# A fourth buffer for the "acc" tiles of an input projection, and late raw tiles placed in the rows pool

## The chip, the cores and the metric

The kernel runs on one core of a Trainium2 chip. The time is the device time of one execution in microseconds (us). The profile is that of one execution; its times count from the start of the recorded span. Engines: PE is TensorE (matrix products), DVE is VectorE, ACT is ScalarE, POOL is GpSimd, and SP is the engine whose queue issues the transfers (DMA).

## The reference

One layer of an encoder block for x of 2048 tokens by 1024 channels, in float32: a pre-norm, one input projection to ten groups of columns, a pooling branch, a bidirectional mLSTM branch, gates, an output projection and a post-norm. Cut to what the change touches:

```python
h = rms_norm(x, norm_pre_g)
proj = jnp.einsum('bsd,de->bse', h, w_in)
u_a, z_a, q, k, v, o, z_b, gates, g_a, g_b = jnp.split(proj, split_points, axis=-1)
pooled = multiscale_pool(u_a)              # window means minus the token, windows 2, 4, 8, 16
y_a = (mix(pooled) * pool_scale) * silu(z_a)
qk = silu(centred_depthwise_conv(concat([q, k]), conv_qk_w, conv_qk_b))   # 5 taps along the tokens
...                                        # mLSTM of q, k, v and the gates, both directions
y_b = hb * sigmoid(o) * silu(z_b)
merged = sigmoid(g_a + b_merge[0]) * (y_a @ w_proj_pool) + sigmoid(g_b + b_merge[1]) * (y_b @ w_proj_mlstm)
out = x + rms_norm(merged @ w_out, norm_post_g)
```

## The kernel before

The function `phase1` is the input projection. It goes over the tokens in two halves of 1024 and, in each, over 36 pairs of 128-column blocks (q, k, v, pooled u, gates z, o and others, by head or group). A pair's product with the half of the tokens is done by Strassen's scheme: seven products, each of 12 matmuls of 128x512 (4 blocks of depth times 3, as each factor is split in a high and a low part). The sums gather in PSUM banks A, B and C, two of each. In `strassen`, S2·T2 goes to a bank B; DVE reads it (L395, tile `u2`); S3·T3 is added in the same bank; DVE reads it again (L400, `u3`); A22·T4 is added, and DVE's L705 or L595 adds the bank to `p1` (to tiles `p` or `raw`). So PE can't go on in the bank until L395, then L400, are done. The products of neighbouring pairs are interleaved: PE runs S3·T3 of a pair 8 us after its S2·T2 ended.

What follows a pair depends on its kind. All of these take tiles of the tag "acc", 128 partitions by up to 1048 floats, from one ring of three buffers:

- `conv` (q, k): ACT writes acc = bias + tap 0 (L623), DVE adds four taps (L628), ACT takes the sigmoid (L632), POOL multiplies (L633), SP stores (L634, to qT or kT).
- `pair_v`: two tiles `vnh` and `vnl` for each half of the pair, with MEMSETs (L647, L648) at their first use, PE transposes (L654, to `vtr`), ACT's and DVE's split into high and low part (L94, L98), and SP's stores.
- `pair_u`: window sums `win` (L685) and `pooled` (L689 to L695).
- `pair_o` and `pair_z`: gate tiles `gB` (L754 to L760) and `zs` (L719 to L724).

A tile of the ring is handed out when the tile three places earlier has been released, that is, when its last reader is done: for a convolution, when its store has landed.

In the second half, convolutions are left over from the first: the second block of each q and k pair needs tokens of both halves, so its raw values were spilled. `late_load` brings one back into a tile `late` (a MEMSET, L638, and a load, L639), and `conv` is run on it after a later pair that is no q, k, u or v. Its taps are tied by `issue_after` to the bank reads of that pair, so that bank reads and taps alternate on DVE. There are eight: q0, k0, q1, k1, q2, k2, q3, k3.

Ahead of the seventh pair of the second half, `row_math` computes the row factors of the mLSTM in the tile `rows`, of tag "rb" in the pool `self.rows` (one buffer).

The order on each engine is not written out by hand: a scheduler sets it from the priorities in the code (`tc.high_priority`, `issue_after`) and from when it reckons tiles to come free. Engines run their instructions in that order.

Of the kernel before, what the change touches and what calls it, by code (L numbers as in the profile page):

```python
# [8 lines left out]
F32 = mybir.dt.float32  # L9
# [4 lines left out]
P = 128  # L14
# [3 lines left out]
HALF = S // 2  # L18
# [54 lines left out]
def run(steps):  # L73
    for _ in steps:
        pass


class Kernel:
# [358 lines left out]
    def phase1(self):  # L437
        tc, nc, a = self.tc, self.nc, self.a
        with ExitStack() as es:
# [7 lines left out]
            po = {t: es.enter_context(tc.tile_pool(name=f"po_{t}", bufs=3)) for t in ("raw", "acc", "p")}  # L447
            self.rows = es.enter_context(tc.tile_pool(name="rows", bufs=1))
            self.decay = es.enter_context(tc.tile_pool(name="decay", bufs=1))
            self.late = es.enter_context(tc.tile_pool(name="late", bufs=1))  # L450
            psum = es.enter_context(tc.tile_pool(name="ps1", bufs=2, space=bass.MemoryType.PSUM))

            class PoolP:
                def tile(s_, shape, dt, tag, name, bufs=None):
                    return po.get(tag, po["p"]).tile(
                        shape, dt, tag=tag, name=name, bufs=bufs or (6 if tag == "p" else 3)
                    )

            pool = PoolP()
# [2 lines left out]
            late, waits = [(kind, h) for h in range(NH) for kind in "qk"], None  # L462
            for half in range(2):
                H = {}
                ops = self.operands(half, H, hp, wc, pool, psum)
                def load(i):
                    return [self.load_w(wr, i, slice(4 * j, 4 * j + 4)) for j in range(2)]

                def work(i, W):
                    return self.pair(half, self.pairs[i], H, W, psum, pool)  # L470


                self.half = half
                W = [{}, {}]
                ahead = lambda: tc.high_priority(offset=NEXT if half else 0)
                with ahead():
                    next(ops)
                    raw = [self.load_w(wr, i, slice(0, 4)) for i in range(2)]
                    if half == 0:
                        raw.append(self.load_w(wr, 0, slice(4, 8)))  # L480
                    next(ops)
                    for i in range(2):
                        self.plain_w(W[i], wc, raw[i], 1, "pool")
                    next(ops)
                    for i in range(2):
                        if len(raw) < 3 + i:
                            raw.append(self.load_w(wr, i, slice(4, 8)))
                        self.plain_w(W[i], wc, raw[2 + i], 2, "pool")
                    if wg is None:
                        wg = self.prep_wg(pool)  # L490
                    next(ops)
                both = []
                for i in range(2):
                    self.plain = ("AB", ("CC", "AB")[i])
                    both.append(work(i, W[i]))
                    next(both[i])
                self.plain = None
                gates = self.gates(half, H, wg, psum, pool)
                for _ in range(KT):
                    next(gates, None)  # L500
                    for g in both:
                        next(g)
                with tc.issue_after(self.evac.ins):
                    next(ops)
                for _ in range(KT):
                    next(gates, None)
                    for g in both:
                        next(g, None)
                run(gates)
                for g in both:  # L510
                    run(g)
                run(ops)
                rest = iter(())
                for i in range(2, n):
                    if half == 1 and i == 6:
                        self.row_math(psum)
                        mask = self.decay.tile([P, 2, P], F32, tag="mask", name="mask", bufs=1)
                        nc.sync.dma_start(mask, a["mask"])
                    if half == 0 and i == 8:
                        self.stats(1, pool)  # L520
                    self.edge = i == n - 1
                    W = {}
                    with tc.high_priority(offset=200):
                        if half == 0:
                            with tc.issue_after(self.scaled[8].ins) if i == 2 else ExitStack():
                                self.prep_w(W, load(i), wc, wt)
                        else:
                            self.again_w(W, i, wr, wc)
                    if half == 1:
                        with tc.issue_after(self.read.ins):  # L530
                            for u in range(max(0, 8 * (i - 10) // 6), max(0, min(32, 8 * (i - 9) // 6))):
                                self.masked(u, mask)
                    if half == 0:
                        self.keep_w(W, i)


                    this, self.read_banks = work(i, W), []
                    next(this)
                    next(rest, None)
                    next(this)  # L540
                    run(rest)
                    next(this)
                    rest = this
                    if half == 1 and waits is not None and i >= 7 and self.pairs[i][0] not in "qkuv":
                        kind, h, raw = waits
                        self.conv(pool, kind, h, 1, raw, HALF - 2, 0, self.read_banks)
                        waits = None
                    elif half == 1 and waits is None and late and i >= 5:
                        with tc.issue_after(self.read.ins):
                            waits = self.late_load(*late.pop(0))  # L550
                run(rest)
# [82 lines left out]
        nc.sync.dma_start(self.sp[f"{kind}T{h}"][:, i, tstart : tstart + n], acc[:, :n])  # L634

    def late_load(self, kind, h):
        raw = self.late.tile([P, HALF + 2], F32, tag="late", name=self.nm("late"))
        self.nc.vector.memset(raw[:, 0:2], 0.0)  # L638
        self.nc.sync.dma_start(raw[:, 2:], self.sp[f"raw{kind}{h}"])  # L639
        return kind, h, raw  # L640
# [932 lines left out]
```

## Time and profile before

| | |
|---|---|
| runs | 2403.22, 2401.22, 2403.05 us; median 2403.05 |
| profiled execution | 2403.61 us, of which the span is 2401.8 |
| mean granted clock of PE | 0.989 |
| busy share of the span | PE 97%, DVE 62%, POOL 48%, ACT 37% |
| input projection, first half, second half, the rest | about 0 to 780, 780 to 1472, 1472 to 2402 us |

A row of a timeline gives the start, the duration, the engine, the line, the operation, the tiles written and read, their size and number, and in brackets the engine's idle time before it with what ended it. "SPq" is SP's queue issuing a transfer. A row of waits says who waited for which instruction: us in total, times, longest.

### The profile page before, as it was taken

The page shows a single profiled execution, that of the slowest core. Times are in us where ns is not written, and L with a number is a line of the kernel's source. Part 1 is how long each engine was busy: PE and PEld are TensorE (multiplying, and loading weights), DVE is VectorE, ACT ScalarE, POOL GpSimd, SP SyncE. Part 2 cuts the span into 40 slices and gives each one's busy share as a digit, 9 for nine tenths or more (in the row PEclk, how much of TensorE's full clock was granted, in tenths as well). Part 3 has the DMA queues.
Part 4 walks back from the last instruction along what each step waited for, and adds up shares of the span by engine and source line. Part 5 has one row for each costly group of instructions (what it writes and reads, how often), then busy time and mean ns, then how long its engine had stood idle before and what let it go on. Part 6 is the DMA issues. An engine that isn't in the chain of part 4 may idle for free.

```text
span 2401.8 us, 35786 instructions
## 1 busy us (share of the span) xinstructions
PE 2321.7 (97%) x12569; PEld 2004.0 (83%) x12569; DVE 1480.2 (62%) x2495; ACT 895.1 (37%) x1773; POOL 1147.0 (48%) x902
## 2 busy tenths in 40 slices
PE   7999999999999989999999999998999999999998
PEld 5787888888887878787878887997989999999776
DVE  6876676677656465565656434887875333354865
ACT  5434333433344333322322333765764212121442
POOL 4655564555545333554664530554554211233775
PEclk9999999999999999999999999998999999999999
DMA  4467656565673566788777866776666546588763
GB/s 150 176 221 266 225 207 236 201 234 210 235 260 126 185 179 215 250 263 272 241 244 248 267 221 245 236 207 204 198 184 201 187 154 197 184 286 276 253 221 123
DMA packets 303011, 521.63 MB, mean 217 GB/s; under 512 B 27504, under 2 KB 138224, under 8 KB 302832
## 3 DMA queue, kind: packets, MB, share of 16 engines
q1 hardware_dynamic: 302832, 519.35, 65.1%
q8 instruction: 99, 1.62, 0.3%
q14 instruction: 80, 0.66, 0.1%
HBM read 318.45 MB, written 200.80 MB: 216 GB/s over the span
## 4 chain that ended last, share of the span: by engine, by line
PE 67%; DMA 11%; DVE 10%; POOL 4%; issue 4%; ACT 3%; SPq 1%; POOLq 0%; DVEq 0%; ACTq 0%
PE bankB L106 6%; PE bankB L107 6%; PE bankB L108 6%; PE bankC L107 4%; PE bankC L106 4%; PE bankC L108 4%; PE bankA L108 4%; PE bankA L107 4%; PE bankA L106 4%; PE num L1213 4%; DVE acc L628 3%; PE pb L922 2%; PE pb L921 2%; PE pb L923 2%; DMA negM<-nm 2%
## 5 line engine op out<-in xcount | busy, mean ns | idle before, releaser
L98 POOL TENSOR_TENSOR wB21l<-wraw,wB21h 128x512 fp32r<-128x512 f32 x76 | 110.1, 1449 | 223.3 <-ACT wB21h L94 181.0
L1197 POOL TENSOR_TENSOR qs<-q,isc 128x256 f32<-128x256 f32 x120 | 91.1, 761 | 152.5 <-PE num L1213 67.0
L628 DVE SCALAR_TENSOR_TENSOR acc<-raw,conv_w,acc 128x1026 f32<-128x1026 f32 (+1 forms) x96 | 153.3, 1610 | 11.3 <-ACT acc L623 8.9
L98 POOL TENSOR_TENSOR wB22l<-wraw,wB22h 128x512 fp32r<-128x512 f32 x76 | 121.8, 1602 | 73.2 <-ACT wB22h L94 51.5
L923 PE MATMUL pb<-oxs,w_proj_mlstml 128*128 128x256 f32 x512 | 143.8, 281 | 0.0
L922 PE MATMUL pb<-oxs,w_proj_mlstmh 128*128 128x256 f32 x512 | 143.8, 281 | 0.0
L921 PE MATMUL pb<-oxs,w_proj_mlstmh 128*128 128x256 f32 x512 | 143.5, 280 | 0.0
L922 PE MATMUL paps<-pys,w_proj_poolh 128*128 128x256 f32 x512 | 142.7, 281 | 0.3 <-POOL pys L98 0.3
L923 PE MATMUL paps<-pys,w_proj_pooll 128*128 128x256 f32 x512 | 141.4, 281 | 0.0
L921 PE MATMUL paps<-pys,w_proj_poolh 128*128 128x256 f32 x512 | 141.3, 280 | 0.0
L98 POOL TENSOR_TENSOR wB11l<-wraw,wB11h 128x512 fp32r<-128x512 f32 x72 | 105.4, 1464 | 47.6 <-ACT wB11h L94 46.8
L106 PE MATMUL bankB<-A22h,wT4h 128*128 128x512 f32 x272 | 107.1, 394 | 9.5 <-DVE u L400 9.4
L106 PE MATMUL bankC<-S1h,wT1h 128*128 128x512 f32 x272 | 107.0, 393 | 3.4 <-ACT sg L739 3.4
L905 POOL TENSOR_TENSOR nm<-nm,mask 128x256 f32<-128x256 f32 x64 | 63.5, 1007 | 93.1 <-DMA nm<-negM 86.4
L395 DVE TENSOR_TENSOR u<-bankB,p 128x512 f32<-128x512 f32 x76 | 52.1, 686 | 90.4 <-PE bankB L108 78.0
L108 PE MATMUL bankB<-S2h,wT2l 128*128 128x512 f32 x272 | 106.5, 391 | 1.1 <-DVE wT2l L98 1.1
L106 PE MATMUL bankB<-S3h,wT3h 128*128 128x512 f32 x272 | 106.2, 390 | 1.3 <-DVE u L395 1.3
L107 PE MATMUL bankB<-S2l,wT2h 128*128 128x512 f32 x272 | 107.3, 395 | 0.0
L108 PE MATMUL bankC<-S1h,wT1l 128*128 128x512 f32 x272 | 106.9, 393 | 0.0
L107 PE MATMUL bankC<-S1l,wT1h 128*128 128x512 f32 x272 | 106.9, 393 | 0.0
L106 PE MATMUL bankA<-A12h,wB21h 128*128 128x512 f32 x272 | 106.7, 392 | 0.0
L108 PE MATMUL bankB<-A22h,wT4l 128*128 128x512 f32 x272 | 106.6, 392 | 0.0
(443 smaller groups left out, 7751.6 us busy)
## 6 DMA issues: line engine op xcount, KB each, us to landing
wraw<-in_w_in SPq DMA_DIRECT2D x110, 512.0 KB, 4.3
wt<-wT2h SPq DMA_DIRECT2D x34, 256.0 KB, 4.6
wt<-wT1h SPq DMA_DIRECT2D x34, 256.0 KB, 4.4
wt<-wT3h SPq DMA_DIRECT2D x34, 256.0 KB, 3.6
wt<-wT2l SPq DMA_DIRECT2D x34, 256.0 KB, 4.2
wt<-wT1l SPq DMA_DIRECT2D x34, 256.0 KB, 4.4
wt<-wT3l SPq DMA_DIRECT2D x34, 256.0 KB, 3.4
wt<-wT4h SPq DMA_DIRECT2D x34, 256.0 KB, 2.2
```

Source lines behind the costliest of these rows:

```text
L98: return eng.tensor_tensor(lo, x, hi.bitcast(F32), op=ALU.subtract)
L106: nc.tensor.matmul(ps, wh, xh, start=start and kt == 0, stop=False, skip_group_check=True)
L107: nc.tensor.matmul(ps, wh, xl, start=False, stop=False, skip_group_check=True)
L108: nc.tensor.matmul(ps, wl, xh, start=False, stop=stop and kt == 3, skip_group_check=True)
L395: self.read_banks.append(nc.vector.tensor_tensor(u2, bank["B"], p1, op=ALU.add))
L628: nc.vector.scalar_tensor_tensor(acc[:, :n], raw[:, tap : tap + n], self.cw[:, ct, tap : tap + 1], acc[:, :n], op0=ALU.mult, op1=ALU.add,)
L905: nc.gpsimd.tensor_tensor(t[:, d, :, :], t[:, d, :, :], mask[:, d, None, :].to_broadcast([P, 2, P]), op=ALU.add)
L921: nc.tensor.matmul(ps, wh, xh, start=i == 0, stop=False)
L922: nc.tensor.matmul(ps, wh, xl, start=False, stop=False)
L923: nc.tensor.matmul(ps, wl, xh, start=False, stop=i == n)
L1197: nc.gpsimd.tensor_tensor(qs[d], q[:, :, ck], isc[:, d, j % 2, None, :].to_broadcast([P, 2, P]), op=ALU.mult)
L1213: nc.tensor.matmul(pn, qs[d][:, kt, :], state[:, kt, :], start=kt == 0, stop=False)
```

## The change

```diff
-            self.late = es.enter_context(tc.tile_pool(name="late", bufs=1))
...
                     return po.get(tag, po["p"]).tile(
-                        shape, dt, tag=tag, name=name, bufs=bufs or (6 if tag == "p" else 3)
+                        shape, dt, tag=tag, name=name, bufs=bufs or dict(p=6, acc=4).get(tag, 3)
                     )
...
-                    elif half == 1 and waits is None and late and i >= 5:
+                    elif half == 1 and waits is None and late and i >= 7:
                         with tc.issue_after(self.read.ins):
                             waits = self.late_load(*late.pop(0))
...
     def late_load(self, kind, h):
-        raw = self.late.tile([P, HALF + 2], F32, tag="late", name=self.nm("late"))
+        raw = self.rows.tile([P, HALF + 2], F32, tag="rb", name=self.nm("late"))
```

The acc ring has four buffers (4192 bytes more of each partition); the pool of the late tile (4104 bytes) is gone, and late tiles take the buffer in which the rows of `row_math` lay before. The first late load is issued two pairs later, after `row_math`; the other seven loads and all eight late convolutions stay at the same pairs. Tiles of tag "acc" now wait for the release of the tile four places earlier. Lines behind L455 move up by one (L628 becomes L627, L705 becomes L704).

PE's order does not change by a row. The instructions are the same on every engine; some of the first phase stand elsewhere. Two places on DVE:

The late convolution of k2 (tile acc_1738 before), with the bank reads of the pair around it (u2_1762 by L395 and u3_1763 by L400), before:

```order
L395 TENSOR_TENSOR u2_1762_10073<-bankB_1759_10045,p1_1761_10059 128x512
L705 TENSOR_TENSOR p1_1731_9887<-bankB_1729_9873,p1_1731_9887 128x512
L705 TENSOR_TENSOR u2_1732_9901<-bankC_1730_9874,u2_1732_9901 128x512
L628 SCALAR_TENSOR_TENSOR acc_1738_9995<-late_1684_9682,conv_w_376,acc_1738_9995 128x1022
L756 TENSOR_TENSOR gB_1737_9979<-u2_1732_9901,gB_1737_9979 128x512
L628 SCALAR_TENSOR_TENSOR acc_1738_9995<-late_1684_9682,conv_w_376,acc_1738_9995 128x1022 x2
L400 TENSOR_TENSOR u3_1763_10128<-bankB_1759_10045,p1_1761_10059 128x512
L628 SCALAR_TENSOR_TENSOR acc_1738_9995<-late_1684_9682,conv_w_376,acc_1738_9995 128x1022
```

The same place after:

```order
L395 TENSOR_TENSOR u2_1762_10070<-bankB_1759_10042,p1_1761_10056 128x512
L627 SCALAR_TENSOR_TENSOR acc_1738_9992<-late_1684_9679,conv_w_373,acc_1738_9992 128x1022 x2
L704 TENSOR_TENSOR p1_1731_9884<-bankB_1729_9870,p1_1731_9884 128x512
L627 SCALAR_TENSOR_TENSOR acc_1738_9992<-late_1684_9679,conv_w_373,acc_1738_9992 128x1022
L704 TENSOR_TENSOR u2_1732_9898<-bankC_1730_9871,u2_1732_9898 128x512
L627 SCALAR_TENSOR_TENSOR acc_1738_9992<-late_1684_9679,conv_w_373,acc_1738_9992 128x1022
L755 TENSOR_TENSOR gB_1737_9976<-u2_1732_9898,gB_1737_9976 128x512
L400 TENSOR_TENSOR u3_1763_10125<-bankB_1759_10042,p1_1761_10056 128x512
```

Two taps moved ahead of both L705, and all four stand ahead of L400, where one stood behind it.

The late convolution of k1 (acc_1570) and the sets of the values of head 2 (vnh_1622, vnl_1623, vnh_1626), before, from its first two taps on; L395 of this pair (u2_1594) stands ahead of these rows:

```order
L628 SCALAR_TENSOR_TENSOR acc_1570_9030<-late_1537_8860,conv_w_376,acc_1570_9030 128x1022 x2
L705 TENSOR_TENSOR p1_1559_8922<-bankB_1557_8908,p1_1559_8922 128x512
L628 SCALAR_TENSOR_TENSOR acc_1570_9030<-late_1537_8860,conv_w_376,acc_1570_9030 128x1022 x2
L705 TENSOR_TENSOR u2_1560_8936<-bankC_1558_8909,u2_1560_8936 128x512
L756 TENSOR_TENSOR gB_1569_9014<-u2_1560_8936,gB_1569_9014 128x512
L638 MEMSET late_1596_9181 128x2
L400 TENSOR_TENSOR u3_1595_9163<-bankB_1591_9080,p1_1593_9094 128x512
L595 TENSOR_TENSOR raw_1589_9078<-bankC_1592_9081,u3_1595_9163 128x512
L647 MEMSET vnh_1622_9307 128x4x2
```

After:

```order
L627 SCALAR_TENSOR_TENSOR acc_1570_9027<-late_1537_8857,conv_w_373,acc_1570_9027 128x1022 x2
L646 MEMSET vnh_1622_9304 128x4x2
L395 TENSOR_TENSOR u2_1594_9105<-bankB_1591_9077,p1_1593_9091 128x512
L627 SCALAR_TENSOR_TENSOR acc_1570_9027<-late_1537_8857,conv_w_373,acc_1570_9027 128x1022 x2
L704 TENSOR_TENSOR p1_1559_8919<-bankB_1557_8905,p1_1559_8919 128x512
L704 TENSOR_TENSOR u2_1560_8933<-bankC_1558_8906,u2_1560_8933 128x512
L755 TENSOR_TENSOR gB_1569_9011<-u2_1560_8933,gB_1569_9011 128x512
L637 MEMSET late_1596_9178 128x2
L647 MEMSET vnl_1623_9305 128x4x2
L646 MEMSET vnh_1626_9324 128x4x2
L400 TENSOR_TENSOR u3_1595_9160<-bankB_1591_9077,p1_1593_9091 128x512
```

The first set of the values (vnh_1622) moved from behind L400 to ahead of L395, and the next two (vnl_1623, vnh_1626) to ahead of L400. By the ring, vnh_1622 now waits for the store of `pooled`, vnl_1623 for the store of the convolution acc_1570, and vnh_1626 for POOL's product of the two gate tiles gB.

## The prediction

> **What bounds the kernel now.** I read the page first, then the list of waits, the busy time of the input projection in 50-us windows, and last the timelines of single stalls. In the page's first part TensorE has nearly the whole span; the other engines have room on average.
>
> ```profile
> PE 2321.7 (97%) x12569; PEld 2004.0 (83%) x12569; DVE 1480.2 (62%) x2495; ACT 895.1 (37%) x1773; POOL 1147.0 (48%) x902
> ...
> PE bankB L106 <- DVE u L400: 9.4, 4, 3.4
> PE vtr L654 <- DVE vnl L98: 5.2, 1, 5.2
> PE vtr L654 <- DVE raw L595: 2.7, 2, 1.7
> ...
> 1050.00:1100.00 50.00, 50.00 (x222) 41.42 (x221) 32.25 (x34) 11.78 (x19) 22.36 (x15) 1.00 0.74 238
> 1100.00:1150.00 50.00, 47.23 (x216) 38.91 (x215) 31.66 (x41) 16.50 (x24) 26.92 (x21) 1.00 0.79 270
> 1200.00:1250.00 50.00, 46.63 (x199) 38.10 (x198) 31.97 (x32) 11.86 (x18) 38.58 (x22) 0.97 0.70 225
> ```
>
> The waits give microseconds in total, times, longest. A window's row gives its length, then the busy time of PE, PEld, DVE, ACT and POOL, the granted clock, the DMA share and GB/s. In the second half of the input projection (about 780 to 1472 us) the products run back to back, 50.00 busy of 50, except where TensorE waits for a bank that VectorE (DVE) has not read yet. The change touches only buffers of this stage, and both orders hold the same matmuls in the same order, so it can win or lose only at such waits: four for L400 (9.4 us), one for the values' L98 (5.2), two for L595 (2.7). The two windows hold the largest late stalls: 2.77 and 3.37 us idle.
>
> **Part 1: the fourth tile, at the late convolution of k2 (PE stalls at 1226).** The first rows are VectorE, ACT and POOL, then PE, SP with a transfer and the landings of all acc transfers, two windows, and the durations of the four multiply-adds ("taps", L628) of such a convolution.
>
> ```profile
> 1206.66 0.69 DVE L705 TENSOR_TENSOR p<-bankB,p 128x512 f32<-128x512 f32 x1 [1.74 <-PE bankB L108]
> 1218.18 1.28 DVE L628 SCALAR_TENSOR_TENSOR acc<-late,conv_w,acc 128x1022 f32<-128x1022 f32 x1 [8.11 <-ACT acc L623]
> 1219.38 1.79 DVE L756 TENSOR_TENSOR gB<-u,gB 128x512 f32<-128x512 f32 x1
> 1221.10 4.56 DVE L628 SCALAR_TENSOR_TENSOR acc<-late,conv_w,acc 128x1022 f32<-128x1022 f32 x2
> 1225.58 0.68 DVE L400 TENSOR_TENSOR u<-bankB,p 128x512 f32<-128x512 f32 x1
> 1216.90 1.25 ACT L623 ACTIVATE acc<-late,conv_b,conv_w 128x1022 f32<-128x1022 f32 x1 [4.89 <-DMA kT<-acc]
> 1218.80 1.82 POOL L98 TENSOR_TENSOR wB21l<-wraw,wB21h 128x512 fp32r<-128x512 f32 x1 [7.90 <-ACT wB21h L94]
> 1221.30 3.27 POOL L759 TENSOR_TENSOR gB<-gB,gB 128x1024 f32<-128x1024 f32 x1 [0.68 <-POOL wB21l L98]
> 1220.06 0.39 PE L106 MATMUL bankB<-S2h,wT2h 128*128 128x512 f32 x1
> 1222.55 0.39 PE L108 MATMUL bankB<-S2h,wT2l 128*128 128x512 f32 x1
> 1226.31 0.50 PE L106 MATMUL bankB<-A22h,wT4h 128*128 128x512 f32 x1 [3.37 <-DVE u L400]
> 1228.05 0.63 PE L106 MATMUL bankB<-A22h,wT4h 128*128 128x512 f32 x1
> 1207.32 0.32 SPq L634 DMA_DIRECT2D kT<-acc  x1
> 1210.93 0.32 SPq L634 DMA_DIRECT2D kT<-acc  x1
> kT<-acc SPq DMA_DIRECT2D x1, 513.0 KB, 5.9
> DMA to landing us min/median/max: 2.7/4.1/11.2
> 1206.46:1230.61 24.15, 20.78 (x86) 0.94 0.73 228
> 1230.61:1249.65 19.04, 19.04 (x85) 0.99 0.82 271
> L628 DVE SCALAR_TENSOR_TENSOR acc<-late,conv_w,acc x32: 1270/1284/3329, 957.8 to 1322.5; 128x1022 f32<-128x1022 f32 x32
> ```
>
> The chain is plain: the convolution takes an acc tile, ACT's L623 waits until that tile's last user, the kT transfer issued at 1210.93, has landed 5.9 us later, DVE idles 8.11 us, and L400 ends at 1226.26 although PE could have used the bank at 1222.55 + 0.39 = 1222.94. From one first use of wB22h to the next this costs 24.15 - 19.04 = 5.1 us, more than the idle 3.37: matmuls go at 0.63 us instead of 0.39 afterwards and the window's clock is 0.94.
>
> With four tiles the same convolution takes the tile one place older, whose kT transfer was issued at 1207.32. Its landing isn't in the trace; by the row of acc transfers it takes 2.7 to 4.1, or 5.9 like its neighbour, so it lands at 1210.0 to 1213.2, 1211.4 with the median. L623 takes 1.25, so the taps start near 1212.7 (1211.3 to 1214.5). The new order puts all four taps, both L705 (L704 after the change) and L756 ahead of L400. Four taps at the median 1.28 are 5.1; as in this stall (1.28, two in 4.56, and a fourth taken at 1.28 too) they are 7.1. The two bank reads are 0.69 each, L756 0.69 to 1.79, L400 0.68. That is 7.9 to 11.0, and L400 ends at 1220.6 with the fast taps, 1223.7 with the slow, 1225.5 with slow taps and a late landing. The slow tap ran while POOL did L759 (1221.30 to 1224.57), and POOL is idle for 7.90 us ahead of wB21h's row; L759 needs L756 and so comes after the taps in the new order. I take the fast end. The stall goes, **5.1 us saved**; a rest of 1225.5 - 1222.9 = 2.6 us at this stall's own 1.5 per us would leave 1.2, so the ends are 1.2 and 5.1. One read is now behind two taps that stood ahead of all of them: L705 of p, at 1206.66 before. It ends near 1212.7 + 2.6 + 0.7 = 1216.0, and PE needs that bank at 1220.06, so 4 us of slack cover it.
>
> The Trainium skill, "TensorE: Matmul & The Clock Gate", section "What's actually happening", says that an idle window of about 3.4 us halves the array's clock until it has been busy as long again. The trace agrees here: 3.37 us idle is followed by 0.63 us matmuls. By that rule a rest of a stall of 1 or 2 us at this place would cost its idle time alone, and the sum would lose 1 to 2 of the 5.1. The Trainium skill, "SBUF — State Buffer", section "Who interferes with whom", has a DVE instruction with two SBUF inputs wait out a whole GpSimd instruction that reads SBUF; the taps' 1270 and 3329 ns are what it would give, and by it POOL's order settles whether the stall is gone or a rest of it stays.
>
> **Part 2: the same at the late convolutions of k1 and q2, and the split values' sets that now stand ahead of bank reads.**
>
> ```profile
> 1085.49 0.65 DVE L693 TENSOR_TENSOR pooled<-win,ih 128x1 f32<-128x1 f32 x1
> 1087.45 0.69 DVE L395 TENSOR_TENSOR u<-bankB,p 128x512 f32<-128x512 f32 x1 [0.28 <-ACT p L389]
> 1094.44 2.60 DVE L628 SCALAR_TENSOR_TENSOR acc<-late,conv_w,acc 128x1022 f32<-128x1022 f32 x2 [6.30 <-ACT acc L623]
> 1105.40 0.68 DVE L400 TENSOR_TENSOR u<-bankB,p 128x512 f32<-128x512 f32 x1
> 1093.16 1.24 ACT L623 ACTIVATE acc<-late,conv_b,conv_w 128x1022 f32<-128x1022 f32 x1 [5.75 <-DMA pooled<-pooled]
> 1101.37 1.06 ACT L632 ACTIVATE late<-acc 128x1022 f32<-128x1022 f32 x1 [2.54 <-DVE acc L628]
> 1102.57 2.36 POOL L633 TENSOR_TENSOR acc<-acc,late 128x1022 f32<-128x1022 f32 x1 [2.37 <-issue]
> 1088.37 0.38 SPq L695 DMA_DIRECT2D pooled<-pooled  x1
> 1092.33 0.39 PE L106 MATMUL bankB<-S3h,wT3h 128*128 128x512 f32 x1
> 1106.14 0.50 PE L106 MATMUL bankB<-A22h,wT4h 128*128 128x512 f32 x1 [2.77 <-DVE u L400]
> 1086.88:1109.01 22.13, 19.36 (x86) 1.00 0.72 233
> 1148.93:1168.38 19.45, 19.34 (x86) 1.00 0.67 220
> ```
>
> At 1106 (k1) the stall costs 22.13 - 19.04 = 3.1 us. After the change L623 takes the tile that DVE's L693 released at 1086.14, so ACT starts near 1087 and not at 1093.16, and the taps at about 1088.3. But now the values' first set (L647, a MEMSET) takes the tile of the pooled transfer that landed just before 1093.16, by its release of ACT, and it stands on DVE ahead of L395. DVE works in order: L395 runs from about 1093.05 to 1093.75, where it was done at 1088.14, and PE's third product, due at 1092.33, waits 1.5 us. That is a new stall, and I price it at its idle time and the 0.3 by which the old one exceeded its 2.77, 1.8. Behind it two taps (2.6), two reads (1.2) and L756 bring DVE to about 1099; the next sets wait for POOL's L633 (last tap 1096.3, L632 1.06, L633 2.36: 1099.8) and for its kT transfer, which at 4.1 lands at 1104.0. L400 then ends at 1104.8; PE needs it at 1106.14 - 2.77 + 1.5 = 1104.9. So the old stall just goes: 3.1 - 1.8 = **1.3 saved**. At a landing of 5.9 instead of 4.1 it is 1.8 less, -0.5; with a pooled transfer that lands 1.5 us sooner it is 3.1.
>
> At 1165 (q2) the taps waited the same way, and the window of 19.45 shows what that costs: 19.45 - 19.04 = **0.4**, which goes.
>
> **Part 3: what keeps its bound, and the late tiles in the rows pool.**
>
> ```profile
> 861.90 0.07 DVE L647 MEMSET vnh<- 128x8 f32 x1 [9.40 <-DMA qT<-acc]
> 995.99 0.79 DVE L675 COPY raw<-halo_u 128x16 f32<-128x16 f32 x1 [8.30 <-DMA kT<-acc]
> ```
>
> The 5.2 us wait (864) and the wait of 1.7 us (998) come from DVE sitting behind a set of a value tile until a qT or kT transfer lands. A fourth tile only moves which of the sets meets that transfer: the other tile of the same pair is next in the ring and stands at the same row of DVE. So both stay, 0. Of the 9.4 us for L400, 9.4 - 3.4 - 2.8 = 3.2 are left for the waits at 1165 and in the first half of the tokens; the latter has the same four taps and weight subtractions ahead of it as before: 0, and 3.2 is the most that could go.
>
> The first late tile is now loaded after the row mathematics, in its memory. Its MEMSET stands on DVE behind the last taps of the pair after the row mathematics and waits for the row tile's readers, which are transfers and transposes from rows that DVE finished a pair earlier; the load follows on SP, more than a pair's 19 us before the convolution that reads it. So 0, from -1 to 1 if its place on DVE or on SP holds something up. One 512 KB load fewer runs beside the row mathematics, and one MEMSET leaves the kernel's start: both 0.
>
> Sum: 5.1 + 1.3 + 0.4 = 6.8 us. The profiled execution took 2403.61 (span 2401.8), so 2396.8; the median of the runs, 2403.05, lies 0.56 below it, so **2396.3**.
>
> **The rivals.**
> 1. The gain is mostly eaten. Taps meet POOL as they did at 1222, or the older transfer takes 5.9 us, and L400 at k2 is still 1 to 2.6 us late (3.6 to 1.2 of 5.1 saved), while k1 trades one stall for another (-0.5 to 1.3 saved). For it: no trace shows the landing, and the taps' longest is 3329 ns. Against it: POOL's idle time at 1211 to 1218. With the 0.4 of q2 that saves 1.1 to 5.3, or 2398 to 2402.
> 2. Slower: at k1 the sets hold both bank reads. DVE cannot read L400 until the kT transfer lands. If that takes x us from 1099.8, PE idles x - 2.7 in all by L400; at the price of the worst stall here (5.1 for 3.37, 1.5 per us) that outweighs 3.1 + 0.4 + 5.1 from x = 8.4 on. At the longest in the row, 11.2, it costs 12.8 and the time is 2407. For it: two transfers in the rows above did hold such sets for 8 to 9 us. Against it: the queue has nothing else to issue from 1093 to 1100, and the median is half of that.
> 3. The change does nothing: four tiles and the convolutions still bound by something else, so that L623 starts as before. Then k1's new stall is alone, and the time is 2403 to 2405. Against it: in both rows ACT names the transfer of the very tile that is no longer the one taken.
> 4. More: k1's pooled transfer lands early and the first-half stall goes as well: 5.1 + 3.1 + 3.2 = 11.4, or 2391.7.
>
> **How the numbers follow.** Chances: the forecast (2394 to 2398) 0.48, more than that 0.07, rivals 1 and 3 within 0.2% (4.8 us, about what a measurement of this kernel can tell from no change) 0.34, slower by more than that 0.11, where rival 2 meets no gain at k2. So faster 0.55, same 0.34, slower 0.11. The range runs from rival 4's 2392 to 2404, which leaves out the worst of rivals 2 and 3.
>
> **What the changed kernel's profile would show.** Right: no wait of PE near 1226 and 1165; L623 of the late convolutions 5 to 6 us earlier against the products around it; a short wait for L395 near 1093 and none for L400 near 1106; the waits of 5.2 and 1.7 us unchanged; PE's windows from 1200 on at 50.00 and clock 1.00. Wrong: a wait for L400 at k2 with a slow tap ahead of it, a wait over 2 us at k1, or a new wait behind the first late tile's MEMSET, after the row mathematics.

## The result, and the profile after

The changed kernel takes 2387.04 us (median of 4 runs, 2385.5 to 2388.18), the kernel before in the same measurement 2402.14 (4 runs): a ratio of 0.9947, 95% interval 0.9933 to 0.996, or 15.1 us less. Two later measurements (e5, and e11 below) gave 0.995 (0.9932 to 0.9967) and 0.9949 (0.9935 to 0.9963), 11.8 and 12.7 us less. The forecast was 6.8 us less: the right direction, and about half the size.

The profile after, from its first part, the rows for L98, L395, L400 and `raw` in the list of waits up to 1500 us, and the busy time in windows, with the columns of those shown of before. The last three windows are the pairs of the three stalls, cut at the same products as in the prediction; the windows of 50 and 100 us are at the same clock times as before and so hold work that lies 3 to 14 us later in the program.

```profile
PE 2313.3 (97%) x12569; PEld 1998.1 (84%) x12569; DVE 1468.2 (62%) x2495; ACT 898.2 (38%) x1773; POOL 1139.3 (48%) x902
...
PE vtr L653 <- DVE vnl L98: 5.3, 1, 5.3
PE bankB L106 <- DVE u L395: 2.3, 2, 1.8
PE vtr L653 <- DVE raw L594: 1.2, 2, 1.0
PE bankB L106 <- DVE u L400: 0.8, 1, 0.8
...
200.00:300.00 100.00, 100.00 (x451) 82.90 (x449) 68.68 (x85) 42.25 (x71) 58.91 (x39) 1.00 0.68 246
950.00:1000.00 50.00, 50.00 (x230) 41.59 (x229) 28.76 (x38) 16.52 (x24) 29.30 (x21) 1.00 0.80 254
1200.00:1250.00 50.00, 50.00 (x226) 41.46 (x225) 31.39 (x41) 11.57 (x19) 29.65 (x21) 1.00 0.82 272
1081.16:1100.20 19.04, 19.04 (x85) 15.77 (x84) 7.60 (x15) 4.98 (x8) 9.51 (x6) 1.00 0.78 255
1140.13:1159.17 19.04, 19.04 (x86) 15.77 (x84) 11.10 (x13) 7.26 (x11) 12.78 (x10) 1.00 0.80 253
1197.25:1216.29 19.04, 19.04 (x86) 15.77 (x84) 10.71 (x13) 6.42 (x10) 12.80 (x11) 1.00 0.83 254
```

All three pairs now take the bare 19.04 us, so 3.1, 0.4 and 5.1 us are gone. Of the 9.4 us for L400, 0.8 are left, at the end of the projection (1459, and 1473 before). Of the two waits for L395 one lies in the first 115 us and one, 0.6 us, at 1300; none lies at k1, where the prediction had one. The stall in the first half of the tokens and the one at 998 are gone as well: their windows, the first two, are full. The wait of 5.3 for L98 stays.

TensorE's order is the same in both kernels, so the two traces can be laid on each other at the same product (the first use of wB22h in each pair), and the difference of the two starts read off. Where it changes, the change won or lost time:

| stretch that ends at (us, before) | change, us | forecast |
|---|---|---|
| kernel's start | -0.3 | 0 |
| 231.7, stall at 228 | -2.8 | 0 |
| 541.9 | +0.4 | not seen |
| 872.8, stall at 864 | -0.8 | 0 |
| 1010.7, stall at 998 | -1.9 | 0 |
| 1109.0, k1 | -3.1 | -1.3 |
| 1168.4, q2 | -0.4 | -0.4 |
| 1230.6, k2 | -5.1 | -5.1 |
| 1327.9 | +0.9 | not seen |

With steps under 0.25 us this makes -13.6 at the end of the input projection. What follows took 1.8 us less here, and in the second profile of the same kernel 1.0 more, so that part is scatter. The steps for 228, 998, k1, q2 and k2 are the same in that second profile (e5) to 0.01 us; the one at 864 was -1.3 there, and the +0.9 near 1300 did not appear.

### The profile page after: what moved, and what is told of

Same layout as the page of the kernel before. It is cut to its first block, busy times and chain, and to the rows that moved or that the text cites. A ratio compares the mean times of both kernels' runs of the same rounds, so it can differ in the third digit from the quotient of the medians.

```text
span 2386.4 us, 35771 instructions
## 1 busy us (share of the span) xinstructions
PE 2313.3 (97%) x12569; PEld 1998.1 (84%) x12569; DVE 1468.2 (62%) x2495; ACT 898.2 (38%) x1773; POOL 1139.3 (48%) x902
## 4 chain that ended last, share of the span: by engine, by line
PE 79%; DVE 8%; DMA 7%; issue 2%; POOL 2%; ACT 2%; SPq 1%; DVEq 0%; POOLq 0%; ACTq 0%
PE bankB L106 8%; PE bankB L107 8%; PE bankB L108 8%; PE bankA L108 5%; PE bankA L107 5%; PE bankC L107 5%; PE bankA L106 5%; PE bankC L106 5%; PE bankC L108 5%; PE num L1212 3%; PE pb L921 2%; PE pb L922 2%; PE pb L920 2%; PE paps L921 2%; PE paps L922 2%
## 5 line engine op out<-in xcount | busy, mean ns | idle before, releaser
L98 POOL TENSOR_TENSOR wB21l<-wraw,wB21h 128x512 fp32r<-128x512 f32 x76 | 107.6, 1416 | 218.9 <-ACT wB21h L94 178.8
L627 DVE SCALAR_TENSOR_TENSOR acc<-raw,conv_w,acc 128x1026 f32<-128x1026 f32 (+1 forms) x96 | 155.8, 1636 | 10.6 <-ACT acc L622 9.7
L98 POOL TENSOR_TENSOR wB22l<-wraw,wB22h 128x512 fp32r<-128x512 f32 x76 | 116.6, 1535 | 77.8 <-ACT wB22h L94 55.8
L98 POOL TENSOR_TENSOR wB11l<-wraw,wB11h 128x512 fp32r<-128x512 f32 x72 | 108.9, 1513 | 54.4 <-ACT wB11h L94 53.6
L395 DVE TENSOR_TENSOR u<-bankB,p 128x512 f32<-128x512 f32 x76 | 52.2, 687 | 107.8 <-PE bankB L108 95.1
L106 PE MATMUL bankB<-S2h,wT2h 128*128 128x512 f32 x272 | 106.2, 391 | 0.0
L107 PE MATMUL bankB<-S3l,wT3h 128*128 128x512 f32 x272 | 106.0, 390 | 0.0
```

The lines of the kernel that those rows point to most:

```text
L98: return eng.tensor_tensor(lo, x, hi.bitcast(F32), op=ALU.subtract)
L106: nc.tensor.matmul(ps, wh, xh, start=start and kt == 0, stop=False, skip_group_check=True)
L107: nc.tensor.matmul(ps, wh, xl, start=False, stop=False, skip_group_check=True)
L395: self.read_banks.append(nc.vector.tensor_tensor(u2, bank["B"], p1, op=ALU.add))
L627: nc.vector.scalar_tensor_tensor(acc[:, :n], raw[:, tap : tap + n], self.cw[:, ct, tap : tap + 1], acc[:, :n], op0=ALU.mult, op1=ALU.add,)
```

## The experiments

**Which part of the change: e1, the late tiles alone.** The late raw tiles in the rows pool, three acc tiles as before.

```
-            self.late = es.enter_context(tc.tile_pool(name="late", bufs=1))
...
-                    elif half == 1 and waits is None and late and i >= 5:
+                    elif half == 1 and waits is None and late and i >= 7:
...
-        raw = self.late.tile([P, HALF + 2], F32, tag="late", name=self.nm("late"))
+        raw = self.rows.tile([P, HALF + 2], F32, tag="rb", name=self.nm("late"))
```

> Part 2 of the change alone: late tiles in the rows pool and the first late load two pairs later, but the acc ring stays at three tiles. The order is that of the kernel before but for one MEMSET and one load. Theory (all of the gain comes from the ring): same time as before, within 2 us, and the same PE waits: 2.5 us near 228, 1.7 near 998, 2.8 near 1106, 3.4 near 1226. Rival (the row mathematics gains from a 512 KB load fewer beside it, or the ring needs the rest): at least 3 us faster, the step in the region of 780 to 870 us.

Measured: 2398.32 us against 2397.4, ratio 1.000 (0.9987 to 1.0014). The stalls stay, if k1's smaller, as the profile's waits show:

```profile
PE bankB L106 <- DVE u L400: 8.2, 5, 3.8
```

TensorE stands 1.2 us at k1 (2.8 before) and 3.8 at k2 (3.4 before). e7 below, also with three tiles, has 3.4 and 2.2 there, so single profiles of kernels with a ring of three differ by about 2 us at one stall. The move into the rows pool costs and brings nothing; the gain is the fourth tile's.

**Which tiles of the ring: e2, a private tile.** As e1, three tiles in the ring, and one more, in a pool `lacc` of one buffer, that only the late convolutions take. So the ring is as short as before, and only the late convolutions no longer wait for it.

```
-        acc = pool.tile([P, HALF + 2], F32, tag="acc", name=self.nm("acc"))
+        acc = pool.tile([P, HALF + 2], F32, tag="lacc" if ties else "acc", name=self.nm("acc"))
```

> The acc ring stays at three, and the fourth tile serves the late convolutions alone. Theory (with a fourth tile everything that takes tiles of the ring moves up, not only the instruction at the stall; the late convolution is the one that clogs the ring in the second half, the xs tiles do it in the first): the stall near 228 stays (2.5 us idle, 2.8 us), those near 998, 1106, 1165 and 1226 go: 1.9 + 3.1 + 0.4 + 5.1 = 10.5 us faster than before, some 2.8 us slower than the changed kernel. Rival (each stall depends on its own tile's wait alone): 998 stays too, since no late convolution stands at it, and 8.6 us are won.

Measured: 2388.57 against 2397.4, ratio 0.9969 (0.9957 to 0.9982). Steps against before, read as above: k1 -3.1, q2 -0.4, k2 -5.0, 998 -1.35, and 228 +2.2. Waits:

```profile
PE bankB L106 <- DVE u L400: 3.9, 2, 3.1
PE vtr L653 <- DVE raw L594: 1.4, 2, 1.0
```

The 3.1 is the stall at 228, which a ring of three keeps. The time alone, 8.8 us less, would fit the rival's 8.6; the steps don't, since most of the stall at 998 is gone (0.35 us idle are left of 1.69) and the stall at 228 cost 2.2 us more in this profile. So the late convolutions alone account for all but about 1 us of the gains in the second half, most of the one at 998 among them, though nothing at 998 is a late convolution; and the stall at 228 needs the fourth tile in the ring. (On PE e2 has 20 transposes and products of the values' pairs in another order, at 1003 and 1250, behind the wait at 998.)

**Memory for it from elsewhere: e3 and e4.** The changed kernel with two fewer of the weight tiles `wc`, and the same with a fifth acc tile in their place.

```
-            wc = es.enter_context(tc.tile_pool(name="wc", bufs=20))
+            wc = es.enter_context(tc.tile_pool(name="wc", bufs=18))
```

> Control for the next run: the changed kernel with 18 instead of 20 weight tiles. Expected within 0 to 3 us of the changed kernel; no new PE wait on weights over 1 us. If it is slower, the next run is read against this one.

> Five acc tiles, with 18 weight tiles to make room. Theory (what is left of the ring's waits is the one near 862: a value tile's set that waits for the qT transfer and holds DVE): that wait of 5.3 us falls to about 2.9, because DVE then waits for the row transfers at that place; 2 to 3 us faster than the control with 18 weight tiles, nothing else moves. Rival (the ring still holds back much that the waits don't show): 5 us or more.

Measured: e3 2398.88 (1.0015, 0.9998 to 1.0032), e4 2398.33 (1.0003, 0.9992 to 1.0013). Both lose all that the change won. In e3 the stretch around the row mathematics costs 8.9 us more than before, with this as its largest wait, and a new stall after 1244 costs 4.2:

```profile
PE vtr L653 <- DVE vnl L98: 10.3, 1, 10.3
```

The five gains of the fourth tile are there in e3 too (-2.8 at 228, -1.95 at 998, k1, q2 and k2 as above); what is lost is lost elsewhere. I had taken the weight tiles to have slack. But the edit did more than take it away: with 18 tiles the scheduler set another order, on PE too (in places at 30 to 115 us, 690 to 863 and 1650 to 1732 in the clock of the changed kernel), and on VectorE at the row mathematics. Whether the shorter pool or the other order costs the time, these runs don't separate. In e4, which has PE's other order as well, the same wait is 7.7 us, 2.6 less, but other stalls grew (6.8 us after 1244), and no gain is left. What a fifth tile would bring with memory of its own stays open.

**The set that meets a transfer: e6 and e7.** The MEMSETs of the split values' last columns written behind the splits; e6 with four tiles, e7 with three.

```
-            nc.vector.memset(hi[:, :, DH:].bitcast(F32), 1.0)
-            nc.vector.memset(lo[:, :, DH:].bitcast(F32), 0.0)
             for c2 in range(2):
...
                 self.split(hi[:, cc, :DH], lo[:, cc, :DH], ps, "act", "dve")
+            nc.vector.memset(hi[:, :, DH:].bitcast(F32), 1.0)
+            nc.vector.memset(lo[:, :, DH:].bitcast(F32), 0.0)
```

> The changed kernel with the values' two MEMSETs written behind the splits, so that a set never waits for a tile ahead of a bank read. Theory (DVE, in order, is held near 862 by a set that waits for the qT transfer; behind it waits the row mathematics for the transfer of its ends, issued at 857 and landing about 2.2 us later): the PE wait of 5.3 us falls to about 2.7, and 2.6 us are won over the changed kernel; nothing at 1106. Rival (the row mathematics' own transfers hold DVE as long): 5.3 us stay, no gain.

> The kernel before, ring of three, with the same edit of the sets alone. Theory: near 864 the wait falls by 2.6 us, near 998 it goes (1.9 us), while 228, 1106, 1165 and 1226, where no set stands ahead of the bank read, stay: 4.5 us faster than before. Rival (998 hangs on the late convolution upstream rather than on the set): 998 stays, 2.6 us.

Measured: e6 2385.91 (0.9955, 0.9938 to 0.9972) beside 2385.48 for the changed kernel on the same chip; e7 2398.01 (1.0003, 0.9992 to 1.0013). No gain in either. VectorE of e6 ahead of the wait near 862, and of e7 ahead of the one at 998, each with its idle time and what ended it:

```profile
858.76 0.36 DVE L860 TENSOR_TENSOR_SCAN rows<-rows 4x16 f32<-4x16 f32 x2 [9.04 <-DMA rows<-ends]
...
994.13 1.23 DVE L675 COPY raw<-halo_u 128x16 f32<-128x16 f32 x1 [7.85 <-POOL acc L633]
```

The set is out of the way in both, and the next instruction in VectorE's order waits as long. In e6 that is the scan of the row mathematics. In e7 it is a copy that waits for POOL's L633: what was late at 998 was a product on POOL, and the kT transfer that the trace of before names only followed it.

**What stands ahead of that: e8, the mask products moved.** The kernel before, with the 32 units of `masked` (loads nm on SP, products L905 on POOL, stores) spread over pairs 23 to 34 and not 10 to 33, so that POOL and SP have none of them at 998, 1106 and 1165.

```
-                            for u in range(max(0, 8 * (i - 10) // 6), max(0, min(32, 8 * (i - 9) // 6))):
+                            for u in range(max(0, 8 * (i - 23) // 3), max(0, min(32, 8 * (i - 22) // 3))):
```

> The kernel before, ring of three, with the 32 loads, POOL products and stores of the masked row factors (nm) moved from the pairs 10 to 33 to the pairs 23 to 34. Theory (the changed kernel lost the waits near 998 and 1106 by more than the tiles' own releases, because stores and loads of nm on SP and the nm products on POOL, in order, had been late): with nm out of the way the store of kT near 991 and that of pooled near 1088 go out 3 to 4 us sooner, and the stalls near 998 (1.9 us) and 1106 (3.1 us) shrink by at least half though the ring has three tiles; 228 and 1226 stay. Later pairs have more nm work, up to 3 us lost there. Rival (only the ring's releases matter): 998 and 1106 stay as they are.

Measured: 2403.83, ratio 1.0025 (1.0013 to 1.0037). Steps: k1 -3.1, q2 -0.4, k2 -3.8, 998 -1.2, with the late convolutions and the ring as they were. But the pair behind the one at 998 loses 1.5, where L400 stands behind slow taps of a late convolution, so nothing is won there in all; and k2, which the theory had unchanged, shrinks too, to 1.0 us idle. It loses more where the units now crowd, 5.8 us at 1252 and 7.2 at 1325. The store of `pooled` that k1's convolution waits for goes out at

```profile
1079.84 0.33 SPq L695 DMA_DIRECT2D pooled<-pooled  x1
```

where it was issued at 1088.37 before; TensorE is 2.9 us ahead there, so the store is 5.6 us earlier against the products. So the stall at k1 had two causes that had to meet: a tile short in the ring, and the mask work ahead of what that tile waits for. Taking away either removes it. At k2 and 998 the smaller waits point the same way, but what the mask work held there was not followed back, and single profiles with a ring of three differ by about 2 us at one stall.

**The wait that stayed: e9, e10 and e12, against e11.** The row mathematics stores `ends`, 128 rows of two floats, reads them back in another order, and scans them. Its second half, from that store on, is queued later: in e9 behind the next weight read on SP; in e10 the same with e6's edit; in e12 a pair later, behind that pair's weight read on SP and behind L395 on VectorE. (The line numbers of e9 and e12 are 5 higher, from the `ends` store on 6.) e12:

```
                     if half == 1 and i == 6:
-                        self.row_math(psum)
+                        rows = self.row_math(psum)
+                        next(rows)
...
+                    if half == 1 and i == 7:
+                        with tc.issue_after(self.read.ins), tc.issue_after(self.read_banks[0].ins):
+                            for _ in rows:
+                                pass
...
+        yield
         nc.sync.dma_start(self.sp["ends"].rearrange("q r -> r q"), ends)
```

> The changed kernel with the second half of the row mathematics, from the store of its `ends` (128 rows of two floats) on, queued on SP behind the next pair's weight read: the qT store (847.78 in the changed kernel) is issued ahead of `ends` and no longer behind it, and on VectorE L400 and the splits stand ahead of the scan L860 that waits for `rows<-ends`. Theory: the small `ends` transfer, 9.2 us, is what makes the qT store behind it land only after 11 us, where the row of acc transfers has a median of 4.1; now that store lands 4 to 6 us after its issue, the values' set (9.38 us behind qT in the changed kernel) and the wait of 5.3 us near 862 go, 4 to 5 us; the chain of `ends` and `carry`, a few us later, may cost 0 to 2 at the scan. In all 2 to 5 us below the changed kernel, no wait for L98 over 1 us. Rival: the qT store takes its 11 us from the weight loads around it, the wait near 862 stays at 4 to 5 us, and the time is that of the changed kernel, or up to 3 us more from the later scan.

> The same, and the MEMSETs of the split value tiles written behind the splits, so that VectorE meets the ring's release only at the split L98 or L653's release. Theory of the run before: the same 2 to 5 us below the changed kernel, at most 0.5 apart from it. Rival: if the qT store lands late by itself, the wait near 862 shrinks here alone, by the 2 us between the set and the split (changed kernel: set 859.00, split 860.93), since the scan no longer holds VectorE.

> The changed kernel, as it is, on the same chip as the two runs before: the measure for them. 2385 to 2389 us, waits as in its first trace (4.4 to 5.3 us for L98 near 862).

> The changed kernel with the second half of the row mathematics, from the `ends` store on, queued a pair later: on SP behind the weight read of the pair after, on VectorE behind the next L395, so that the scan that waits for `rows<-ends` stands 18 instructions behind the four splits L98 of the values and not ahead of them (in the runs e9 and e10 it still stood ahead of the splits, against what their expectation said of the order). Theory: the wait of 4.4 to 5.3 us for L98 near 862 has two holders, the qT store delayed by the `ends` transfer ahead of it and the scan; with both gone the wait goes: 4 to 5 us below the changed kernel, 2380 to 2383, if the scan's own wait (`ends` and back, 9 and 5 us after their issues) holds no bank read in the pair after; if it does, up to 2 of it come back there. Rival: the values' split waits for something third (the qT store by itself, the weight loads), and the wait near 862 stays at 4 us or more; 2385 to 2388.

Measured on one chip: e9 2386.62 (0.9955, 0.994 to 0.997), e10 2386.33 (0.995, 0.9935 to 0.9964), e11, the changed kernel, 2385.54 (0.9949, 0.9935 to 0.9963). So no gain, but not for the rival's reason. SP and VectorE of the changed kernel, with the landing of the qT store; then the same of e9:

```profile
844.54 0.37 SPq L852 DMA_DIRECT2D ends<-rows  x1
847.78 0.32 SPq L633 DMA_DIRECT2D qT<-acc  x1
DMA to landing us min/median/max: 11.2/11.2/11.2
859.00 0.07 DVE L647 MEMSET vnl<- 128x8 f32 x1 [9.38 <-DMA qT<-acc]
```

```profile
846.67 0.32 SPq L638 DMA_DIRECT2D qT<-acc  x1
848.39 0.53 SPq L858 DMA_DIRECT2D ends<-rows  x1
DMA to landing us min/median/max: 2.7/2.7/2.7
849.42 0.07 DVE L652 MEMSET vnl<- 128x8 f32 x1
859.34 0.37 DVE L866 TENSOR_TENSOR_SCAN rows<-rows 4x16 f32<-4x16 f32 x2 [9.26 <-DMA rows<-ends]
```

With `ends` behind it the qT store lands in 2.7 us and not 11.2, and the set no longer waits. That half of the theory held. But the scan stands ahead of the splits here too; the expectation had the order the wrong way round, and VectorE waits 9.26 us for the scan where it waited 9.38 for the set. The split, and TensorE behind it, is as late as it was; e10, without the set, waits 10.6 us for the same scan.

e12 puts the scan behind the splits as well, and takes 2381.05 us against 2397.27: ratio 0.9934 (0.9917 to 0.9951), 16.2 us less than before, where the changed kernel had 11.8 to 15.1. VectorE of e12 at the same place, the largest wait for the values' tile, and the window:

```profile
849.68 0.07 DVE L652 MEMSET vnl<- 128x8 f32 x1
850.98 1.28 DVE L98 TENSOR_TENSOR vnl<-vtr,vnh 128x512 fp32r<-128x512 f32 x2
880.28 0.18 DVE L866 TENSOR_TENSOR_SCAN rows<-rows 4x16 f32<-4x16 f32 x1
...
PE vtr L658 <- DVE raw L599: 1.4, 2, 1.2
...
850.00:900.00 50.00, 49.41 (x225) 40.58 (x224) 28.64 (x45) 20.34 (x34) 19.61 (x11) 1.00 0.76 231
```

The split runs at 850.98 and not at 860.93, and no wait for L98 is left at the vtr tile. Laid on the changed kernel, the stretch to 869 is 6.8 us shorter, the next pair 0.6, and the one behind it 1.6 longer: 5.9 won for a wait of 4.4 to 5.3. That it is more than the wait fits the clock: the changed kernel's three profiles have 3.41 us at a granted clock of 0.5 at this wait, e12 has none. The scan now finds its data landed, as its row shows no wait. e12 is the best version here. It was timed on another chip than the changed kernel, so their difference, about 4 us by the two ratios' distances from before, is less sure than either ratio: the intervals overlap.

## Why the forecast was right in sign and wrong in size

**Part 1, k2: right, in size and cause.** ACT, VectorE and POOL after:

```profile
1198.55 1.24 ACT L622 ACTIVATE acc<-late,conv_b,conv_w 128x1022 f32<-128x1022 f32 x1 [1.09 <-DMA kT<-acc]
1199.82 2.61 DVE L627 SCALAR_TENSOR_TENSOR acc<-late,conv_w,acc 128x1022 f32<-128x1022 f32 x2 [2.92 <-ACT acc L622]
1204.73 1.99 DVE L627 SCALAR_TENSOR_TENSOR acc<-late,conv_w,acc 128x1022 f32<-128x1022 f32 x1
1207.25 0.68 DVE L400 TENSOR_TENSOR u<-bankB,p 128x512 f32<-128x512 f32 x1
1204.35 1.29 POOL L98 TENSOR_TENSOR wB21l<-wraw,wB21h 128x512 fp32r<-128x512 f32 x1 [4.40 <-ACT wB21h L94]
```

The convolution still waits for a kT transfer, but an older one. TensorE is 9.2 us ahead at this place, so the taps' start of 1199.8 is 1209.0 in the clock of before: 9.2 us ahead of the 1218.18 there, not 5.5 (the forecast's 1212.7). Three taps take the fast 1.3 us. One takes 1.99, beside POOL's L98 from 1204.35 to 1205.64, which is the slow tap of rival 1 at a fraction of its price; L400 ends at 1207.93, and TensorE wants the bank at 1222.94 - 9.21 = 1213.7, so 5.8 us of slack hide it. With the stall the low clock goes too (1.00 in the window).

**Part 2, q2: right; k1: the term 3.1 - 1.8 = 1.3 was mis-sized.** It measured 3.1, since the new wait for L395 did not come. SP and VectorE after:

```profile
1078.46 0.38 SPq L694 DMA_DIRECT2D pooled<-pooled  x1
1083.07 0.07 DVE L646 MEMSET vnh<- 128x8 f32 x1 [1.75 <-DMA pooled<-pooled]
1083.12 0.69 DVE L395 TENSOR_TENSOR u<-bankB,p 128x512 f32<-128x512 f32 x1
1093.55 0.07 DVE L647 MEMSET vnl<- 128x8 f32 x1 [2.97 <-DMA kT<-acc]
1094.13 0.68 DVE L400 TENSOR_TENSOR u<-bankB,p 128x512 f32<-128x512 f32 x1 [0.52 <-issue]
```

The sets stand where the order put them, and the first holds VectorE for the store of `pooled`, as forecast. But the step that failed is that I took this store's time, 1088.37, from the trace of before. It goes out 9.9 us sooner, of which TensorE's lead explains 5.7: 4.2 us earlier against the products, where 1.5 would have done. So the third product finds its bank free: L395 ends at 1083.8, and TensorE comes to it at 1092.3 - 5.7 = 1086.6. The prediction named the case ("a pooled transfer that lands 1.5 us sooner it is 3.1") and gave it 0.07 together with the stall at 228. The second set holds L400 as well; kT lands 3.5 us after its issue (1090.04 to 1093.55), L400 ends at 1094.8, and TensorE wants it at 1103.4 - 5.7 = 1097.7 (1103.4 is 1106.14 less the idle 2.77), so rival 2 has nothing to act on.

Where the 4.2 us come from is read by following the store back. On POOL, `win` (L685, after the change L684) works behind the mask products, these wait for the loads nm, the loads stand on SP behind the store of zs, that waits for VectorE's L720, and L720 stands behind the taps of q1's late convolution. Before, then after (where the products' own wait ends with a weight load):

```profile
1060.61 1.78 DVE L720 TENSOR_TENSOR zs<-u,zs 128x512 f32<-128x512 f32 x1
1064.92 0.45 SPq L724 DMA_DIRECT2D zs<-zs  x1
1065.90 1.56 SPq L901 DMA_DIRECT2D nm<-negM  x2
1073.21 1.43 POOL L905 TENSOR_TENSOR nm<-nm,mask 128x256 f32<-128x256 f32 x2 [8.41 <-DMA nm<-negM]
1074.60 1.91 POOL L685 TENSOR_TENSOR win<-raw 128x1034 f32<-128x1034 f32 x1
```

```profile
1051.58 0.69 DVE L719 TENSOR_TENSOR zs<-u,zs 128x512 f32<-128x512 f32 x1 [0.69 <-ACT zs L718]
1052.30 0.92 SPq L723 DMA_DIRECT2D zs<-zs  x1
1056.07 1.35 SPq L900 DMA_DIRECT2D nm<-negM  x2
1063.00 1.42 POOL L904 TENSOR_TENSOR nm<-nm,mask 128x256 f32<-128x256 f32 x2 [7.06 <-DMA wraw<-in_w_in]
1064.38 1.91 POOL L684 TENSOR_TENSOR win<-raw 128x1034 f32<-128x1034 f32 x1
```

q1's late convolution is itself one of those that take an older tile: its taps start at 1039.0 and not at 1050.6, 5.8 us earlier against the products. Each late convolution freed from its wait brings forward what queues behind it on three engines, and so what the next one waits for. e2 shows that the late convolutions alone do this, and e8 that the stall needs the mask work in the middle of this chain.

**Part 3: "so both stay, 0" failed at 998.** The sentence that the other tile of the same pair meets that transfer is true, but it took the transfer's own time as fixed. It also read the row as that of a set; the row is L675's copy into a `raw` tile, which POOL's L633 reads. The chain of POOL, before and after:

```profile
982.16 1.50 POOL L905 TENSOR_TENSOR nm<-nm,mask 128x256 f32<-128x256 f32 x1 [5.70 <-DMA nm<-negM]
989.04 2.40 POOL L633 TENSOR_TENSOR acc<-acc,raw 128x1026 f32<-128x1026 f32 x1
```

```profile
974.85 0.74 POOL L904 TENSOR_TENSOR nm<-nm,mask 128x256 f32<-128x256 f32 x1 [4.94 <-DMA nm<-negM]
981.85 2.40 POOL L632 TENSOR_TENSOR acc<-acc,raw 128x1026 f32<-128x1026 f32 x1
```

L633 and the kT store behind it are 7.2 us sooner, 3.7 of it the lead TensorE had: 1.9 us won, and e7 had the same L633 as the end of the wait. At 864 the forecast held in size, as the wait stays (5.3, and 4.4 in two further profiles), but with some luck: it named one holder, the set, and e9 to e12 show a second, the scan.

**The stall at 228: "the same four taps and weight subtractions ahead of it as before: 0" failed.** The same taps and subtractions stand ahead of L400, but they start earlier. TensorE and ACT before, then ACT after:

```profile
228.80 0.50 PE L106 MATMUL bankB<-A22h,wT4h 128*128 128x512 f32 x1 [2.52 <-DVE u L400]
217.01 1.06 ACT L166 ACTIVATE xs<-xs 128x1024 f32<-128x1024 f32 x1 [2.45 <-DMA xs<-in_x]
218.07 1.23 ACT L623 ACTIVATE acc<-raw,conv_b,conv_w 128x1022 f32<-128x1022 f32 x1
```

```profile
213.10 1.24 ACT L622 ACTIVATE acc<-raw,conv_b,conv_w 128x1022 f32<-128x1022 f32 x1 [1.23 <-DVE raw L594]
```

The input tiles xs lie in the same ring. With four tiles their load comes sooner, ACT's L166 no longer stands waiting in front of the convolution, and the convolution starts 4.6 us earlier against the products. e1 and e2, with three tiles in the ring, keep the stall, with 2.1 and 3.1 us idle. The forecast had not counted these tiles among the users of the ring. Its 3.2 us left for 1165 and the first half were 2.5 here, 0.8 at the end of the projection, which stayed, and no idle at 1165.

**The late tiles in the rows pool and one load less: 0, right** (e1, ratio 1.000). The loss of 0.4 at 526, where TensorE stands 0.19 us before the transposes of values, was not foreseen; it came again in the later profiles of the changed kernel, and its cause stays open.

So three terms were too small for the same reason, k1 by 1.8, 998 by 1.9 and 228 by 2.8: the arrivals that they hung on were read from the trace of before and held fixed. The outcome is rival 4 in kind, and it had 0.07. Its 11.4 us and the 1.9 at 998 make 13.3, close to the 13.6 of the input projection. It deserved more: each piece of it hung on transfers whose times were read from a trace in which the same ring had delayed them.

## What to carry to other kernels

A buffer added to a ring moves every step that takes a tile from it, and then all that queues in order behind those steps on every engine and DMA queue. Before a later stall is priced with the old arrival times, follow what it waits for back two or three steps: if one of them stood behind the ring, it arrives sooner too. And where a set and a scan both hold the same engine for transfers, removing one alone shows nothing (e6, e9, e10); move them together (e12).

## What the runs showed of the hardware

- The store of `ends`, 128 rows of two floats, delays a store of 513 KB issued 3.2 us behind it on the same queue to 11.2 us; with the order of the two turned round (e9, e10), or `ends` a pair later (e12), that store lands in 2.7. The weight store wT3h, next behind `ends` in the changed kernel, took 9.2 us as well, the one ahead of it, wT1l, 4.0. So the small transfer was the dear one. Why so few bytes do this no run shows.
- The price of a stall isn't its idle time alone. 2.77 us idle at k1 gave back 3.1 when they went, 3.37 at k2 gave back 5.1. Behind the second the granted clock is 0.5 for 3.41 us, behind the first it stays 1.00. The length of the idle time does not settle which of the two follows: in e7 only 2.17 us idle at k2 are followed by 3.41 us at 0.5 and cost 4.0 in all, in e2 the 3.11 at 228 likewise and cost 5.0. So a stall that lowers the clock cost 1.7 to 1.9 us above its idle time here. The Trainium skill, "TensorE: Matmul & The Clock Gate", section "What's actually happening", puts the bound at an idle window of about 3.4 us. The 2.77 and the 3.37 would fit that; the 2.17 of e7 does not, so a rest of a stall can cost more than the idle time at which the prediction priced it by that rule.
- Two `wc` weight tiles fewer, with the other order that came with them, cost about 13 us by the medians (2398.88 against the 2385.5 of other measurements), although TensorE waits for no weight tile longer than 1.2 us in the input projection of the changed kernel. Which of the two makes the larger stalls stays open.
